# The second layer's attention: weights times values for four token tiles in one product, gate weights loaded block by block

## The chip, the cores and the metric

One Trainium2 chip, one of its cores. The kernel is one launch; its time is the device time of that launch in microseconds. TensorE (PE in the profile) multiplies, VectorE (DVE), ScalarE (ACT) and GpSimd (POOL) do the elementwise work, and SyncE (SP) issues most of the DMAs. Each engine takes its instructions in the order in which the program lists them.

## The reference, cut to what matters

Two layers work on 512 latent and 256 context tokens of width 1024. The change lies in the second layer, which is grouped-query attention with 8 query heads of width 128 and 2 key/value heads:

```
h = rms_norm(x) * (1 + scale) + shift
q, k, v, z = split(h @ w_in)
q, k = rope(rms_norm(q)), rope(rms_norm(k))
p = softmax(q @ k.T * scale)        # per head: 512 queries, 768 keys
o = p @ v                           # per head: 512 x 128
x = x + gate * rms_norm((o * silu(z)) @ w_out)
gate = silu(c) @ ada_w[..., 2D:3D] + b
```

All inputs are float32. The kernel keeps nearly that precision by splitting each factor into a high and a low part and summing three products (high by high, high by low, low by high).

## The kernel before, in words

**Stages of the second layer.** After keys and values are ready, the kernel runs one long stretch in which eight heads of attention, four query projections (`q_proj`, two heads each) and eight gate projections (`z1_proj`, one head each) are interleaved. The projections are the filler: generators in a queue, from which the planner `flow` draws a few products whenever no attention step is due.

**One head.** A *unit* of scores (`s1_units`) takes one tile of 128 tokens. PE makes six products of 384 columns into one of two PSUM buffers, `sc0` and `sc1`. DVE takes the row maximum (L1537) and multiplies it by the query's norm (L1540); ACT exponentiates and sums (L1543); DVE takes the reciprocal of the sum (L1544); POOL scales the tile (L233). The result is a tile of weights `p`, 128 tokens by 768 keys, of which there are 5 buffers.

**Weights times values.** `pv1_steps` works on *two* token tiles at a time (a half, `ch` 0 or 1), so each head goes through it twice. A `tstep` transposes four 128x128 blocks (two token tiles, two key blocks) into one PSUM bank `bk` (L1558); ACT casts them to the high part `ah` (L1561) and DVE forms the low part `al` (L1562). An `mstep` then does the products of this step (`pv_mm`, L167): three terms by two key blocks, six products of 256 columns. Three steps make a half, so a head has 36 such products. At the end of each half ACT copies 128x256 out of the bank (L1575). There are three buffers each of `ah` and `al` (`AB`).

**Banks.** Four banks `bk0` to `bk3` serve projections, transposes and value products in turn; a bank is free again when its reader on ACT or DVE is done.

**Gate.** `gate` of the second layer is formed on DVE: 16 blocks (8 blocks of the inner dimension by two halves of 512 columns) are multiplied by a column of silu(c) and accumulated (L1602, L1604). `gate1_load` fetches two blocks per DMA, 512 KB, into one of two buffers `gw` (L1589); it is issued on SP, where the projections' weights (L223) are issued too. `gate1_finish` sums over the partitions on PE (L406, L407).

**Who sets the order.** Steps have lags and due times (`SLAG1`, `QLAG`, `QTR`, `LA`, `LT`, `LM`, `AT1`, `TS`), a model clock, and priorities (`HOT1`, one per stream). `flow` writes steps in order of their due times; the scheduler below it then orders each engine's queue by priority and readiness.

Of the kernel before, what the change touches and what calls it, by code (L numbers as in the profile page):

```python
# [33 lines left out]
ACD = 0.54  # L34
FILL1 = (('q', 1), ('z', 0), ('z', 2), ('q', 2), ('z', 1), ('q', 3), ('z', 4), ('z', 5), ('z', 3), ('z', 6), ('z', 7))
HOT0 = (4682, 2421, 950, 3759)
HOT1 = (1476, 3151, 2600, 3663, 2938, 0)
WARM = 1817
AGB = 10
PRE = 16.26  # L40
# [13 lines left out]
LT = (1.27, 1.44)  # L54
AHEAD = 2
SLAG = (4.74, 1.08)
SLAG1 = 4.72
AT1 = 12.82
EGL = 'v'
EXS = 'pvvvvv'  # L60
EHF = ('vvvvvvpv', 'pvvvvvvv')
# [6 lines left out]
PRI = (1500, 218, 582, 400)  # L68
GFIN = (10, 13)
QLAG = 2.87  # L70
QTR = 5.35
EG0 = 'v'
EP0 = 'p'
EN1 = 'p'
# [13 lines left out]
def tile_backbone(  # L88
# [1289 lines left out]
    with tc.tile_pool(name="t1", bufs=1, side="right") as t1p:  # L1378
# [126 lines left out]
                pieces(nc.gpsimd, gT1[h], gT1[h], szt1[h], ALU.mult)  # L1505

        def z1_proj(h):
            while not ws.has(12 + h):
                yield None
            wh, wl = ws.get(12 + h)  # L1510
            o = pj(512)
            for kt in range(KT):
                mm3(o, gcols(wh, kt), gcols(wl, kt), h1hi[:, kt, :512], h1lo[:, kt, :512], kt == 0, kt == KT - 1)
                yield 3 * 512 / 2400.0
            ws.release(12 + h)
            sz = t1q.tile([P, 512], F32, tag="sz", name=nm("sz"), bufs=2)
            nc.scalar.copy(sz, o)
            close(o)
            za = t1q.tile([P, 512], F32, tag="za", name=nm("za"), bufs=1)
            silu_parts(sz, za, sz, nc.gpsimd)  # L1520
            szt1[h] = sz
            gate_mul1(h)

        def s1_units(h, ms):
            res = []

            def unit(m):
                g = h // 4
# [8 lines left out]
                nc.vector.tensor_reduce(mx, scv, AX.XY, ALU.max, negate=True)  # L1537
                sr = qrs[h // 2, m][:, h % 2:h % 2 + 1]
                nmx = small()
                nc.vector.tensor_tensor(nmx, mx, sr, ALU.mult)  # L1540
                pt = t1q.tile([P, T], F32, tag="p", name=nm("p"), bufs=5)
                l = small()
                nc.scalar.activation(pt.rearrange("p (j n) -> p j n", j=2), scv, AF.Exp, scale=sr, bias=nmx, accum_out=l)  # L1543
                nc.vector.reciprocal(l, l)  # L1544
                scaled(EN1, pt, pt, l)
                res.append(pt)
# [3 lines left out]
        def pv1_steps(h, at, ch, after, ts, ms):  # L1550
# [31 lines left out]

            chunk(1, tstep, mstep, (0, 2, 4), [after], ts, ms)

        gws = {}

        def gate1_load(half, k2):
            gw = gws[half, k2] = t1q.tile([P, 1024], F32, tag="gw", name=nm("gw"), bufs=2)
            nc.sync.dma_start(  # L1589
                gw.rearrange("p (k n) -> p k n", k=2),  # L1590
                ada_w[1, k2 * 256:(k2 + 1) * 256, 2 * D + half * 512:2 * D + half * 512 + 512].rearrange("(k p) n -> p k n", p=P),
            )

        def gate1_part(half, k2):
            acc = gate1[:, half * 512:half * 512 + 512]
            gw = gws.pop((half, k2))
            with tc.issue_after(last_of(nc.vector)):
                for k in range(2):
                    kt = k2 * 2 + k
                    gs = gw[:, k * 512:(k + 1) * 512]  # L1600
                    if kt == 0:
                        nc.vector.tensor_scalar(acc, gs, scol[:, 0, kt:kt + 1], None, ALU.mult)  # L1602
                    else:
                        nc.vector.scalar_tensor_tensor(acc, gs, scol[:, 0, kt:kt + 1], acc, ALU.mult, ALU.add)  # L1604

        def gate1_finish(half):
            acc = gate1[:, half * 512:half * 512 + 512]
# [38 lines left out]
            add(out_head(o_pre, ghi, glo, w_o[0], OUTC1[0][1]))  # L1646

        at_ = clock[0] + AT1
        qtr = {}
        for h in range(KT):  # L1650
            p, j = h // 2, h % 2
            lag = [(S_[4 * (h - 1) - 1], QLAG)] if h >= 2 else []
            qtr[h] = Step(lambda p=p, j=j: q_tr(p, j), 0.44, lag, ready=lambda p=p: q_t[p] + QTR if p in q_t else None)
            X_.append(qtr[h])
            for ch in range(2):
                at, u = s1_units(h, (2 * ch, 2 * ch + 1))
# [13 lines left out]
        for i in range(8):  # L1670
            if i >= 0:
                Z_.append(Step(lambda i=i: gate1_load(i // 4, i % 4), 0.0, [(S_[1 + i], 0.0)], hot=False))
            if i:
                Z_.append(Step(lambda i=i: gate1_part((i - 1) // 4, (i - 1) % 4), 0.0, [(S_[1 + i + 1], 0.0)], hot=False))
        Z_.append(Step(lambda: gate1_part(1, 3), 0.0, [(S_[1 + 9], 0.0)], hot=False))
# [140 lines left out]
```

## Time and profile before

| | |
|---|---|
| time, median of 3 runs | 792.78 us (792.57 to 792.84) |
| the profiled execution's own time | 792.77 us |
| its span, first to last instruction | 790.8 us |
| lies outside the span | 2.0 us |
| granted TensorE clock | 0.999 |
| PE, DVE, ACT, POOL busy | 98%, 66%, 58%, 41% |
| the second layer's attention, from the first score to the last value product | about 577.4 to 753.2 us |

How to read it: the page is one execution. Busy PE time is the union of overlapping products, so a product's own duration (0.28 us for 256 columns) is longer than the time from its start to that of the next. What a product costs a dense stream is that distance, and the chain of waits gives it: it lists stretches of back-to-back work with their count. A wait of PE appears as "idle before" in the timeline and in the table of waits.

### The profile page before, as it was taken

The page shows a single profiled execution, that of the slowest core. Times are in us where ns is not written, and L with a number is a line of the kernel's source. Part 1 is how long each engine was busy: PE and PEld are TensorE (multiplying, and loading weights), DVE is VectorE, ACT ScalarE, POOL GpSimd, SP SyncE. Part 2 cuts the span into 40 slices and gives each one's busy share as a digit, 9 for nine tenths or more (in the row PEclk, how much of TensorE's full clock was granted, in tenths as well). Part 3 has the DMA queues.
Part 4 walks back from the last instruction along what each step waited for, and adds up shares of the span by engine and source line. Part 5 has one row for each costly group of instructions (what it writes and reads, how often), then busy time and mean ns, then how long its engine had stood idle before and what let it go on. Part 6 is the DMA issues. An engine that isn't in the chain of part 4 may idle for free.

```text
span 790.8 us, 14236 instructions
## 1 busy us (share of the span) xinstructions
PE 776.8 (98%) x5446; PEld 699.2 (88%) x5446; DVE 522.4 (66%) x940; ACT 455.4 (58%) x994; POOL 324.9 (41%) x434
## 2 busy tenths in 40 slices
PE   8999999999999999999999999999999999999996
PEld 6688888988887898888979998899999999989986
DVE  4666677786769637866578753567558977565634
ACT  5546546675575644775468843565456676676632
POOL 1121375663338542353425411585446654234101
PEclk9999999999999999999999999999999999999999
DMA  9934211131422322323330151041423512010102
GB/s 339 384 97 148 80 54 59 50 104 67 138 80 83 118 81 68 120 80 107 117 97 31 51 213 54 1 140 53 159 82 101 153 43 81 27 54 28 54 27 107
DMA packets 35092, 77.77 MB, mean 98 GB/s; under 512 B 3408, under 2 KB 10064, under 8 KB 35024
## 3 DMA queue, kind: packets, MB, share of 16 engines
q1 hardware_dynamic: 31168, 71.05, 26.9%
q10 hardware_dynamic: 3856, 5.81, 2.1%
q8 instruction: 43, 0.70, 0.3%
q14 instruction: 25, 0.20, 0.1%
HBM read 70.56 MB, written 2.10 MB: 92 GB/s over the span
## 4 chain that ended last, share of the span: by engine, by line
PE 89%; DVE 3%; ACT 3%; DMA 2%; POOL 1%; issue 1%; SPq 0%; DVEq 0%; ACTq 0%; POOLq 0%
PE bk L155 56%; PE sc L155 10%; PE bk L167 9%; PE sc L994 5%; PE bk L1059 3%; PE bk L1558 3%; PE bk L835 1%; DMA xnt<-in_xlT 1%; PE sc L1023 1%; POOL wlo L219 1%; DMA raw<-in_b_w 1%; DVE al L1063 1%; PE bk L406 1%; PE bk L407 1%; ACT p L1033 0%
## 5 line engine op out<-in xcount | busy, mean ns | idle before, releaser
L155 PE MATMUL bk<-whi,h 128*128 128x256 f32 (+1 forms) x1184 | 243.7, 299 | 0.0
L155 PE MATMUL bk<-h,whi 128*128 128x512 f32 (+2 forms) x864 | 227.9, 347 | 0.0
L155 PEld LDWEIGHTS bk<-whi,h 128*128 128x128 f32 x1184 | 191.8, 191 | 10.5 <-issue 4.0
L155 PE MATMUL bk<-wlo,h 128*128 128x256 f32 (+1 forms) x592 | 175.7, 299 | 0.0
L155 PEld LDWEIGHTS bk<-h,whi 128*128 128x128 f32 x864 | 149.9, 189 | 17.1 <-issue 2.9
L155 PE MATMUL bk<-h,wlo 128*128 128x512 f32 (+2 forms) x432 | 149.6, 346 | 0.0
L233 POOL TENSOR_SCALAR p<-p,sm 128x768 f32<-128x768 f32 (+1 forms) x80 | 71.7, 899 | 163.1 <-DVE sm L1005 63.9
L155 PEld LDWEIGHTS bk<-wlo,h 128*128 128x128 f32 x592 | 112.6, 191 | 3.8 <-issue 0.7
L219 DVE TENSOR_TENSOR wlo<-raw,whi 128x1024 fp32r<-128x1024 f32 (+1 forms) x66 | 80.7, 1226 | 34.4 <-ACT whi L225 34.3
L155 PEld LDWEIGHTS bk<-h,wlo 128*128 128x128 f32 x432 | 81.5, 189 | 7.1 <-issue 0.2
L225 ACT CAST whi<-raw 128x1024 fp32r<-128x1024 f32 x64 | 67.2, 1050 | 32.9 <-PE bk L155 27.8
L1002 ACT ACTIVATE p<-sc,sm 128x768 f32<-128x768 f32 (+1 forms) x68 | 59.5, 878 | 30.6 <-DVE sm L999 30.1
L999 DVE TENSOR_REDUCE sm<-sc 128x1 f32<-128x768 f32 (+1 forms) x68 | 60.3, 917 | 19.2 <-PE sc L994 19.2
L219 POOL TENSOR_TENSOR sz<-sz,za 128x192 f32<-128x192 f32 (+1 forms) x48 | 35.1, 752 | 65.8 <-ACT za L199 65.7
L1010 DVE SCALAR_TENSOR_TENSOR p<-p,sm,p 128x768 f32<-128x768 f32 (+1 forms) x34 | 40.3, 1186 | 7.4 <-POOL p L233 5.1
L994 PE MATMUL sc<-qk,qk 64*128 64x384 f32 (+1 forms) x396 | 43.8, 351 | 0.7 <-ACT p L1002 0.7
L1562 DVE TENSOR_TENSOR al<-bk,ah 128x512 fp32r<-128x512 f32 x48 | 32.1, 686 | 18.4 <-ACT ah L1561 18.2
L1062 ACT CAST ah<-bk 128x512 fp32r<-128x512 f32 x56 | 31.6, 589 | 19.0 <-PE bk L1059 16.6
L1063 DVE TENSOR_TENSOR al<-bk,ah 128x512 fp32r<-128x512 f32 x56 | 37.4, 683 | 6.7 <-ACT ah L1062 6.5
L1543 ACT ACTIVATE p<-sc,sm,qrs 128x768 f32<-128x768 f32 x32 | 31.9, 996 | 15.1 <-DVE sm L1540 8.9
L994 PEld LDWEIGHTS sc<-qk,qk 64*128 64x128 f32 x396 | 32.8, 184 | 7.7 <-issue 3.4
L1561 ACT CAST ah<-bk 128x512 fp32r<-128x512 f32 x48 | 26.9, 588 | 17.9 <-PE bk L1558 14.6
(240 smaller groups left out, 1492.6 us busy)
## 6 DMA issues: line engine op xcount, KB each, us to landing
raw<-in_a_w SPq DMA_DIRECT2D x28, 512.0 KB, 3.5
araw<-in_ada_w SPq DMA_DIRECT2D x12, 1024.0 KB, 5.2
raw<-in_b_w SPq DMA_DIRECT2D x20, 512.0 KB, 3.5
ag<-in_ada SPq DMA_DIRECT2D x16, 512.0 KB, 7.9
raw<-in_w_out SPq DMA_DIRECT2D x16, 512.0 KB, 3.5
sw<-qr ACTq DMA_DIRECT2D x32, 128.0 KB, 2.1
gw<-in_ada_w SPq DMA_DIRECT2D x8, 512.0 KB, 4.1
xnt<-in_xlT SPq DMA_DIRECT2D x4, 512.0 KB, 5.6
```

What stands on the lines that cost most here:

```text
L155: i = nc.tensor.matmul(o, a, b, start=start, stop=stop)
L167: nc.tensor.matmul(o, v[:, kt + e, c], a[:, e * 256:e * 256 + 256], start=first and i == 0, stop=last and i == 5)
L219: eng.tensor_tensor(dst[:, i:i + n], a[:, i:i + n], b[:, i:i + n], op)
L225: nc.scalar.copy(hi, r)
L233: (nc.vector if eng == "v" else nc.gpsimd).tensor_scalar(dst, src, s_, 1.0, ALU.mult, ALU.mult)
L994: prev = nc.tensor.matmul(sc[m][:, j if nk == T else m, :w], a[r, tok], b[r, c], start=i == 0, stop=i == 2)
L999: nc.vector.tensor_reduce(mx, scv, AX.XY if nk == T else AX.X, ALU.max, negate=True)
L1002: nc.scalar.activation(pv_, scv, AF.Exp, bias=mx, accum_out=l[:, m:m + 1])
L1010: nc.vector.scalar_tensor_tensor(ps_[0], pt, r, ps_[0], ALU.mult, ALU.add)
L1063: nc.vector.tensor_tensor(al, tr, f32(ah), ALU.subtract)
L1543: nc.scalar.activation(pt.rearrange("p (j n) -> p j n", j=2), scv, AF.Exp, scale=sr, bias=nmx, accum_out=l)
L1562: nc.vector.tensor_tensor(al, tr, f32(ah), ALU.subtract)
```

## The change

**Value products.** For heads 0 to 6 a new function, `pv1_wide`, replaces `pv1_steps`. It waits for all four units of the head. A `tstep` transposes one key block of all four token tiles (four blocks of 128x128, as before, L1592) and splits it into `ah` and `al` (L1595, L1596), a step of 128x512 as before; there are six such steps, one per key block. An `mstep` does three products of 512 columns (L1606). A head thus has 18 products of 512 columns in place of 36 of 256, one copy of 128x512 out of the bank (L1609) in place of two of 128x256, and the same 24 transposes, 6 casts and 6 subtractions. Head 7 keeps the two halves.

**Buffers and order.** `p` has 7 buffers instead of 5, since four tiles of a head are held until all are there. A unit now waits in the planner for the last transposes of the head whose `p` buffer it takes over. `z1_proj` does not start while two gated heads are waiting for their attention. The planner's constants move: `HOT1[4]`, `SLAG1`, `AT1`, `QTR`, `LM[1]`.

**Gate loads.** A load is one block, 256 KB, into one of two buffers of half the size. The first two loads are issued ahead of the attention; each further one follows the accumulation of the block whose buffer it takes. The 16 accumulations are the same.

```diff
-HOT1 = (1476, 3151, 2600, 3663, 2938, 0)
+HOT1 = (1476, 3151, 2600, 3663, 3405, 0)
...
-QTR = 5.35
+QTR = 6.73
...
         def z1_proj(h):
-            while not ws.has(12 + h):
+            while not ws.has(12 + h) or sum(g not in done1 for g in szt1) >= 2:
                 yield None
...
-                pt = t1q.tile([P, T], F32, tag="p", name=nm("p"), bufs=5)
+                pt = t1q.tile([P, T], F32, tag="p", name=nm("p"), bufs=7)
...
+        def pv1_wide(h, at, after, ts, ms):
+            g = h // 4
+            st = {}
+
+            def tstep(kt):
+                tr = trp()
+                for i, a in enumerate(at):
+                    nc.tensor.transpose(tr[:, i * P:(i + 1) * P], a[:, kt * P:(kt + 1) * P], ident)
+                ah = t1q.tile([P, 512], F32R, tag="ah", name=nm("ah"), bufs=AB)
+                al = t1q.tile([P, 512], F32R, tag="al", name=nm("al"), bufs=AB)
+                nc.scalar.copy(ah, tr)
+                nc.vector.tensor_tensor(al, tr, f32(ah), ALU.subtract)
+                st[kt] = ah, al
+
+            def mstep(kt):
+                if kt == 0:
+                    st["o"] = pj(512)
+                o = st["o"]
+                ah, al = st[kt]
+                c = slice(g * P, (g + 1) * P)
+                for i, (v, a) in enumerate(((vh, ah), (vl, ah), (vh, al))):
+                    nc.tensor.matmul(o, v[:, kt, c], a, start=kt == 0 and i == 0, stop=kt == NT - 1 and i == 2)
...
+            chunk(1, tstep, mstep, range(NT), [after], ts, ms)
...
-            gw = gws[half, k2] = t1q.tile([P, 1024], F32, tag="gw", name=nm("gw"), bufs=2)
...
+            gw = gws[half, kt] = t1q.tile([P, 512], F32, tag="gw", name=nm("gw"), bufs=2)
+            nc.sync.dma_start(gw, ada_w[1, kt * P:(kt + 1) * P, 2 * D + half * 512:2 * D + half * 512 + 512])
...
-                    if len(T_) >= 6:
-                        st_.lag.append((T_[-4], 0.0))
+                    used = (len(S_) - 7) // 4
+                    if used >= 0:
+                        st_.lag.append((tl[used], 0.0))
...
+        for i in range(2):
+            gate1_load(0, i)
+        for i in range(16):
+            Z_.append(Step(lambda i=i: gate1_part(i // 8, i % 8), 0.0, [(S_[1 + i // 2], 1.5 * (i % 2))], hot=False))
+            if i < 14:
+                Z_.append(Step(lambda i=i: gate1_load((i + 2) // 8, (i + 2) % 8), 0.0, [(Z_[-1], 0.0)], hot=False))
```

Nothing ahead of the second layer's attention moves. Three places within it show how the queues change.

**PE, between heads 4 and 5.** In these rows `p` is a tile of weights, `q` a tile of queries, `sc` a buffer of scores, `h1` with `whi` and `wlo` a product of a gate projection. Before, around the transposes of head 4's second half and the queries' transposes:

```order
L155 MATMUL bk2_70<-h1_687_5281,wlo_1050_7414 128x512
L1558 MATMUL bk0_68<-ident_74,p_1122_7793 128x128
L1494 MATMUL bk1_69<-ident_74,q_1073_7542 128x128
...
L1558 MATMUL bk0_68<-ident_74,p_1128_7843 128x128
L1558 MATMUL bk0_68<-ident_74,p_1122_7793 128x128
L1558 MATMUL bk0_68<-ident_74,p_1128_7843 128x128
L155 MATMUL bk2_70<-h1_687_5281,whi_1049_7413 128x512
L155 MATMUL bk2_70<-h1_688_5282,whi_1049_7413 128x512
L155 MATMUL bk2_70<-h1_687_5281,wlo_1050_7414 128x512
```

The same place in the changed program, where head 3's last steps meet head 4's first (`p_1171` is head 4's fourth tile):

```order
L1606 MATMUL bk2_70<-ah_1167_7938,vl_5916 128x512
L1592 MATMUL bk1_69<-ident_74,p_1171_7952 128x128
L1592 MATMUL bk0_68<-ident_74,p_1139_7789 128x128
L1592 MATMUL bk0_68<-ident_74,p_1145_7818 128x128
L1592 MATMUL bk0_68<-ident_74,p_1150_7840 128x128
L1592 MATMUL bk0_68<-ident_74,p_1171_7952 128x128
L1606 MATMUL bk2_70<-al_1168_7939,vh_5915 128x512
L155 MATMUL sc1_73<-kh_5913,qh_1141_7801 128x384
L155 MATMUL sc1_73<-kl_5914,qh_1141_7801 128x384
```

Gate projections stood between the attention steps before. Now PE's rows 4202 to 4314 hold no projection at all: 30 products of scores (five units), 39 transposes of weights, 8 of queries and 36 value products.

**ACT, at head 2's fourth tile.** `ah` is the cast after a transpose, `za` and `sz` belong to the silu of a gate projection. Before, the exponential of that tile (`p_1057`):

```order
L195 ACTIVATE za_1052_7419<-sz_1051_7417 128x512
L196 ACTIVATE za_1052_7419<-za_1052_7419 128x512
L1543 ACTIVATE p_1057_7457,sm_1058_7458<-sc0_72,sm_1056_7455,qrs_909_6730 128x768
L197 ACTIVATE za_1052_7419<-za_1052_7419 128x512
L1575 COPY g1_1036_7348<-bk1_69 128x256
L1561 CAST ah_1053_7443<-bk0_68 128x512
```

and now (`p_1083`):

```order
L197 ACTIVATE za_1071_7484<-za_1071_7484 128x512
L1595 CAST ah_1063_7455<-bk3_71 128x512
L199 ACTIVATE za_1071_7484<-za_1071_7484 128x512
L1543 ACTIVATE p_1083_7537,sm_1084_7538<-sc0_72,sm_1082_7535,qrs_911_6734 128x768
L1595 CAST ah_1065_7472<-bk3_71 128x512
```

The exponential now stands behind a cast (`ah_1063`) that itself waits for head 1's transposes on PE.

**DVE, at the last gate blocks.** `gw` is a block's buffer, `al` the low part of a step. Before, two accumulations read one buffer:

```order
L1562 TENSOR_TENSOR al_1038_7355<-bk0_68,ah_1037_7354 128x512
L1604 SCALAR_TENSOR_TENSOR gate1_5280<-gw_1005_7214,scol_109,gate1_5280 128x512
L1537 TENSOR_REDUCE sm_1055_7453<-sc0_72 128x1
L1544 RECIPROCAL sm_1044_7388<-sm_1044_7388 128x1
L1604 SCALAR_TENSOR_TENSOR gate1_5280<-gw_1005_7214,scol_109,gate1_5280 128x512
L1562 TENSOR_TENSOR al_1040_7374<-bk3_71,ah_1039_7373 128x512
```

and now each reads its own, with the loads of `gw_1030` and `gw_1042` issued after the 13th and the 14th block (`gw_1011` and `gw_1014`):

```order
L1629 SCALAR_TENSOR_TENSOR gate1_5280<-gw_1014_7207,scol_109,gate1_5280 128x512
L1540 TENSOR_TENSOR sm_1046_7366<-sm_1045_7364,qrs_893_6640 128x1
L1629 SCALAR_TENSOR_TENSOR gate1_5280<-gw_1030_7280,scol_109,gate1_5280 128x512
L1544 RECIPROCAL sm_1048_7369<-sm_1048_7369 128x1
L1498 TENSOR_TENSOR ql_1044_7336<-bk2_70,qh_1043_7335 128x512
L1629 SCALAR_TENSOR_TENSOR gate1_5280<-gw_1042_7328,scol_109,gate1_5280 128x512
L1537 TENSOR_REDUCE sm_1054_7414<-sc1_73 128x1
L1596 TENSOR_TENSOR al_1051_7385<-bk0_68,ah_1050_7384 128x512
```

Behind the last block stand the maximum of head 2's third unit and head 1's first `al`. On SP, weights of later projections are queued behind these loads.

More of the change, by code (lines that the diff above doesn't have):

```diff
@@ L56 @@
 SLAG = (4.74, 1.08)
-SLAG1 = 4.72
-AT1 = 12.82
+SLAG1 = 5.06
+AT1 = 13.45
 EGL = 'v'
@@ L78 @@
 RL = 3.57
-LM = (4.64, 5.5)
+LM = (4.64, 6.57)
 AB = 3
@@ L1583, in pv1_steps @@
             chunk(1, tstep, mstep, (0, 2, 4), [after], ts, ms)
-        gws = {}
-        def gate1_load(half, k2):
-            gw = gws[half, k2] = t1q.tile([P, 1024], F32, tag="gw", name=nm("gw"), bufs=2)
[L1589 to L1594, printed above, removed]
+        def pv1_wide(h, at, after, ts, ms):
[18 more added lines that the diff above has]
+                    nc.tensor.matmul(o, v[:, kt, c], a, start=kt == 0 and i == 0, stop=kt == NT - 1 and i == 2)
+                if kt == NT - 1:
+                    gT1[h] = t1p.tile([P, 512], F32, tag="g1", name=nm("g1"), bufs=8)
+                    (nc.scalar.copy if EG1 == "a" else nc.vector.tensor_copy)(gT1[h], o)
+                    close(o)
+                    done1.add(h)
+                    gate_mul1(h)
+            chunk(1, tstep, mstep, range(NT), [after], ts, ms)
@@ L1595, in gate1_part, with gate1_load @@
+        gws = {}
+        def gate1_load(half, kt):
+            gw = gws[half, kt] = t1q.tile([P, 512], F32, tag="gw", name=nm("gw"), bufs=2)
+            nc.sync.dma_start(gw, ada_w[1, kt * P:(kt + 1) * P, 2 * D + half * 512:2 * D + half * 512 + 512])
+        def gate1_part(half, kt):
             acc = gate1[:, half * 512:half * 512 + 512]
-            gw = gws.pop((half, k2))
+            gs = gws.pop((half, kt))
             with tc.issue_after(last_of(nc.vector)):
[L1598 to L1604, printed above, removed]
+                if kt == 0:
+                    nc.vector.tensor_scalar(acc, gs, scol[:, 0, kt:kt + 1], None, ALU.mult)
+                else:
+                    nc.vector.scalar_tensor_tensor(acc, gs, scol[:, 0, kt:kt + 1], acc, ALU.mult, ALU.add)
@@ L1648, in tile_backbone @@
         at_ = clock[0] + AT1
-        qtr = {}
+        qtr, tl = {}, {}
         for h in range(KT):
@@ L1654, in tile_backbone @@
             X_.append(qtr[h])
-            for ch in range(2):
-                at, u = s1_units(h, (2 * ch, 2 * ch + 1))
+            wide = h < KT - 1
+            for ch in range(1 if wide else 2):
+                at, u = s1_units(h, range(NQ) if wide else (2 * ch, 2 * ch + 1))
                 for i, st_ in enumerate(u):
@@ L1661, in tile_backbone @@
                         st_.lag.append((S_[-2], SLAG1))
-                    if len(T_) >= 6:
-                        st_.lag.append((T_[-4], 0.0))
+                    used = (len(S_) - 7) // 4
+                    if used >= 0:
+                        st_.lag.append((tl[used], 0.0))
                     S_.append(st_)
-                if h == KT - 1 and ch == 1:
+                if not wide and ch == 1:
                     T_.append(Step(tail1, 0.0, [(M_[-1], 0.0), (u[-1], 0.0)]))
-                pv1_steps(h, at, ch, u[-1], T_, M_)
+                if wide:
+                    pv1_wide(h, at, u[-1], T_, M_)
+                    tl[h] = T_[-1]
+                else:
+                    pv1_steps(h, at, ch, u[-1], T_, M_)
         Y_ = [Step(lambda i=i: gate1_finish(i), 0.9, [(S_[GFIN[i]], 0.0)], hot=False) for i in range(2)]
         Z_ = []
[L1670 to L1675, printed above, removed]
+        for i in range(2):
[4 more added lines that the diff above has]
+                Z_.append(Step(lambda i=i: gate1_load((i + 2) // 8, (i + 2) % 8), 0.0, [(Z_[-1], 0.0)], hot=False))
         flow(1, [S_, T_, M_, X_, Z_, Y_])
```

## The prediction

> **What bounds the kernel now.** I began with the page: busy shares, then the chain that ended last.
>
> ```profile
> PE 776.8 (98%) x5446; PEld 699.2 (88%) x5446; DVE 522.4 (66%) x940; ACT 455.4 (58%) x994; POOL 324.9 (41%) x434
> PE 89%; DVE 3%; ACT 3%; DMA 2%; POOL 1%; issue 1%; SPq 0%; DVEq 0%; ACTq 0%; POOLq 0%
> ```
>
> PE is busy for 98% of the span and carries 89% of the chain. Two stretches of the second layer's attention, and the table of waits of PE from 573 to 785 us, say how dense it is there. The columns of the stretches are length, then busy time of PE, PEld, DVE, ACT and POOL with their instructions, granted clock, DMA share, GB/s.
>
> ```profile
> 592.30:660.00 67.70, 67.70 (x504) 66.04 (x503) 58.35 (x113) 44.92 (x103) 39.82 (x48) 1.00 0.31 95
> 660.00:760.00 100.00, 99.56 (x659) 92.28 (x658) 59.56 (x108) 62.67 (x123) 31.02 (x39) 1.00 0.13 43
> ...
> PE sc L155 <- ACT p L1543: 0.4, 1, 0.4
> ```
>
> PE waits once in 212 us. DVE has 9 us to spare in the first 68, so its results come just in time there, yet PE doesn't feel it. So time is won here only by less work on PE, and lost only where PE is made to wait. The timeline of PE shows the one wait (start, duration, what):
>
> ```profile
> 704.75 0.27 PE L1558 MATMUL bk<-ident,p 128*128 128x128 f32 x1
> 705.46 0.44 PE L155 MATMUL sc<-kh,qh 128*128 128x384 f32 x1 [0.44 <-ACT p L1543]
> ```
>
> From the transpose's start to the next product's are 0.71 us; a transpose takes a dense stream 0.11 (below), so PE loses 0.60.
>
> **The products.** What a product costs a dense stream I read from the chain in order of time (start, us, what and how many), and the number of value products from their line:
>
> ```profile
> 643.15 1.91 PE bk L167 x16
> 645.07 0.44 PE bk L1558 x4
> 645.50 1.04 PE sc L155 x6
> 646.78 1.92 PE bk L155 x16
> ...
> 668.28 4.59 PE bk L155 x20
> ...
> 709.76 4.61 PE bk L155 x20
> ...
> L167 PE MATMUL bk<-ah,vh x96: 278/283/367, 606.7 to 752.4; 128*128 128x256 f32 x96
> ```
>
> The 16-fold stretches are products of 256 columns, 1.91 / 16 = 0.1194 and 1.92 / 16 = 0.120 us each; the 20-fold ones have 512 columns, 0.2295 and 0.2305. There are 96 for each of three terms, 288 in eight heads, 36 a head. Seven heads give up 252 x 0.1194 = 30.1 us and get 126 x 0.2295 = 28.9: a gain of 1.2. With the other rows it is 252 x 0.1194 - 126 x 0.2305 = 1.05 to 252 x 0.120 - 126 x 0.2295 = 1.3. It lies on PE, so all of it counts unless a wait eats it. Transposes (0.11 each) and score units (1.04) stay as many.
>
> [...]
>
> The copies out of the bank (two of 128x256 become one of 128x512), the seven `p` buffers and the planner's constants cost PE nothing themselves; ACT is not the bound.
>
> **The old wait.** The 0.60 us hung on an exponential late on ACT for a buffer of scores. The changed order has other neighbours there; I count it as gone, and its like under the new waits.
>
> **New waits.** Three places could make PE wait. The durations, from the groups of the lines between 573 and 785 us and of POOL between 590 and 750 (busy us, mean ns, idle before):
>
> ```profile
> L1543 ACT ACTIVATE p<-sc,sm,qrs 128x768 f32<-128x768 f32 x32 | 31.9, 996 | 15.1 <-DVE sm L1540 8.9 <-PE bk L1558 3.4 <-POOL qrs L1411 2.1
> L1561 ACT CAST ah<-bk 128x512 fp32r<-128x512 f32 x48 | 26.9, 588 | 17.9 <-PE bk L1558 14.6 <-PE bk L167 3.0
> L1543 ACT ACTIVATION_READ_ACCUMULATOR p<-sc,sm,qrs 128x1 f32 x32 | 6.4, 199 | 0.0
> L195 ACT ACTIVATE za<-sz 128x512 f32<-128x512 f32 x8 | 5.1, 639 | 0.2
> ...
> L1562 DVE TENSOR_TENSOR al<-bk,ah 128x512 fp32r<-128x512 f32 x48 | 32.1, 686 | 18.4 <-ACT ah L1561 18.2
> L1537 DVE TENSOR_REDUCE sm<-sc 128x1 f32<-128x768 f32 x32 | 30.4, 949 | 2.0 <-PE sc L155 1.7
> L219 DVE TENSOR_TENSOR wlo<-raw,whi 128x1024 fp32r<-128x1024 f32 x18 | 22.9, 1272 | 13.9 <-ACT whi L225 13.9
> L1540 DVE TENSOR_TENSOR sm<-sm,qrs 128x1 f32<-128x1 f32 x32 | 7.4, 232 | 0.3
> ...
> L1544 DVE RECIPROCAL sm<-sm 128x1 f32<-128x1 f32 x30 | 4.7, 158 | 11.0 <-ACT p L1543 10.9
> ...
> L233 POOL TENSOR_SCALAR p<-p,sm 128x768 f32<-128x768 f32 x31 | 31.9, 1028 | 55.0 <-DVE sm L1544 40.8 <-DVE sm L1540 10.4 <-PE bk L406 3.7
> ```
>
> An engine starts the next instruction before the last has ended. Timelines of ACT and of DVE show by how much:
>
> ```profile
> 664.23 0.60 ACT L1561 CAST ah<-bk 128x512 fp32r<-128x512 f32 x1
> 664.71 1.01 ACT L1543 ACTIVATE p<-sc,sm,qrs 128x768 f32<-128x768 f32 x1
> ...
> 643.57 0.95 DVE L1537 TENSOR_REDUCE sm<-sc 128x1 f32<-128x768 f32 x1
> 644.43 0.68 DVE L1562 TENSOR_TENSOR al<-bk,ah 128x512 fp32r<-128x512 f32 x1
> ```
>
> A cast of 0.60 us holds ACT for 0.48, a maximum of 0.95 holds DVE for 0.86: about 0.1 less than the duration. Each place is bounded by full durations and by these steps.
>
> *The stretch without projections*, PE's rows 4202 to 4314. It is PE work of 5 x 1.04 + 47 x 0.11 + 36 x 0.2295 = 18.6 us, with nothing to fill a wait. ACT's rows for it are 6 exponentials with their sums (7.2), 11 casts (6.5), 2 copies of a cast's size (1.2), 4 activations of the silu (2.6) and one cast of 128x1024 for which I take two of 512 (1.2): 18.7 us, or about 16 with the overlap. DVE has 6 maxima (5.7), 10 `al` and one `ql` (7.5), 11 small ones (2.2), one `wlo` (1.3) and one step of the silu (0.8): 17.5, or 15. At full durations both are as long as PE's work and hand results back and forth; walking the rows I find two waits, 0.3 us at head 4's second transposes (bank 0, for `al_1168`) and 0.6 at its fourth (bank 1, for `al_1189`). With the overlap both vanish, a microsecond to spare. So 0 to 0.9; the overlap is measured, the hand-overs between engines are not in it, and I take 0.4.
>
> *Head 2's fourth tile* (`p_1083`). Its exponential stands on ACT behind `ah_1063`, which needs transposes of head 1. From their end to the fourth tile's transpose, PE has 11 transposes, 5 value products and one unit: 1.2 + 1.15 + 1.04 = 3.4 us. The chain is cast, silu step, exponential, sum, reciprocal, scaling: 0.59 + 0.64 + 1.0 + 0.2 + 0.16 + 1.03 = 3.6, and the first cast starts about 0.2 after the transposes; overlapped it is 3.3 to 3.4. So a wait of 0.1 to 0.4, and the `ah_1065` behind it is late by as much: I take 0.4 for both.
>
> *Gate blocks on DVE.* A DVE instruction that waits for a block holds up the maxima and `al` behind it. I take 0.1 here on the likely case, and make the rest a rival. What else is late on SP (later projections' weights behind the loads) has tens of microseconds.
>
> **The sum.** 792.77 (the profiled execution, 790.8 in its span and 2.0 around it; the median is 792.78) - 1.2 - 0.6 + 0.4 + 0.4 + 0.1 = 790.97 + 0.9 = 791.9 us. A difference under 0.2%, 1.6 us, is about what a measurement of this kernel can't tell from no change; so faster means below 791.2 and slower above 794.4.
>
> **Rivals.**
>
> *No new wait at all.* PE stays as dense as before: 790.97, say 791.0, 0.23% faster. For it speaks that before, with DVE idle for 18 us at the casts (`L1562`'s row), PE still waited only once; the order allows it, with at least 7 us of PE's work between a unit's products and the transposes of its tile. Against it: the stretch without filler has no parallel in the trace. It decides if all waits together stay under 0.2 us or so.
>
> *The gate blocks hold up DVE, and PE with it.* The rows of the loads:
>
> ```profile
> L1604 DVE SCALAR_TENSOR_TENSOR gate<-gw,scol,gate x14: 725/742/1291, 597.6 to 638.5; 128x512 f32<-128x512 f32 x14
> L1589 SPq DMA_DIRECT2D gw<-in_ada_w x8: 368/379/464, 555.6 to 628.0; - x8
> DMA to landing us min/median/max: 3.8/4.1/5.0
> ...
> raw<-in_ada_b SPq DMA_DIRECT2D x4, 256.0 KB, 3.8
> ```
>
> 512 KB land 4.1 us after issue, another tile's 256 KB 3.8. A block is loaded only when the one two places ahead has been accumulated: 0.38 to issue and 3.8 to land, 4.2 us. In DVE's order four instructions lie between the 14th block and the 16th, 0.23 + 0.74 + 0.16 + 0.68 = 1.8 us, so DVE may wait 2.4 there; between the 5th and the 7th are six, about 2.5 us, a wait of up to 1.7. If PE pays both in full, the time is 791.0 + 4.1 = 795.1, slower. It decides where the `al` and maxima behind those blocks are needed sooner than these waits; the rows give them some microseconds, since projections still stand between at these places, and before the change DVE waited long without PE noticing. [...]
>
> *The wide product is no cheaper.* If 512 columns cost just twice 256 in this place, the first term is 0, and the time 791.9 + 1.2 = 793.1: no change. The rows at 643 and 668 us speak against it, though they are of different stretches. [...]
>
> **Chances.** Forecast 0.44, no new wait 0.32, wide product no cheaper 0.06, gate blocks or a like hold-up 0.18. So faster 0.32, same 0.50, slower 0.18. The range of the forecast alone is 790.97 - 0.1 (upper gain) + 0 to 2.3 (all three places at their upper ends, with 1 us for the gate blocks), 790.9 to 793.3. To hold 8 in 10 it has to reach into the rival on either side: 790.7 to 794.6.
>
> **What would show it.** The span's PE order should give 18-fold value products at 0.23 us each in the chain; 126 products of L1606 with 128x512; PE's table of waits in the attention near 0.9 us in all, and naming ACT `ah` or POOL `p` at head 2 and a DVE `al` at heads 4 and 5. I am wrong if the end of the last value product moves by other than -0.9 us against 753.2 (the work behind it is the same), if PE's waits name `gate`, or if DVE stands idle for a DMA `gw` by more than 2 us and PE's gaps follow it.

## The result, and the profile after

The changed kernel takes 795.38 us, median of 6 runs (795.14 to 795.85), beside 792.72 (792.39 to 793.29) for the kernel before on the same chip: a ratio of 1.0034, 95% interval 1.0024 to 1.0044. It is slower by 2.7 us. The profiled span is 793.9 us, 3.1 longer than before's.

The shares by engine and the chain, from the page of after:

```profile
PE 777.3 (98%) x5320; PEld 691.0 (87%) x5320; DVE 521.3 (66%) x940; ACT 454.5 (57%) x987; POOL 324.8 (41%) x434
PE 87%; ACT 3%; DVE 3%; DMA 2%; POOL 2%; issue 2%; SPq 0%; DVEq 0%; ACTq 0%; POOLq 0%
```

PE has 126 products fewer, as planned, and is busy just as long; its share of the chain fell by two points, which went to POOL and to "issue". The two stretches of the attention, then PE's table of waits from 573 to 788 us:

```profile
592.30:660.00 67.70, 65.66 (x426) 59.73 (x425) 55.24 (x107) 41.89 (x96) 39.42 (x48) 1.00 0.36 110
660.00:760.00 100.00, 99.78 (x593) 88.42 (x593) 61.27 (x113) 64.86 (x122) 30.75 (x38) 1.00 0.12 38
```

```profile
PE sc L155 <- ACT p L1543: 1.1, 3, 0.6
PE bk L407 <- POOL ac L405: 0.9, 1, 0.9
```

The loss is in the first stretch. PE was busy for all of its 67.70 us before and lacks 2.04 now, at the same granted clock of 1.00; the second stretch is denser than before's 99.56. The table counts only time in which no product was running. What a wait costs shows in the distance from a product's start to the next one's, less that product's own step in a dense stream (0.109 us for a transpose, 0.120, 0.175 and 0.229 for 256, 384 and 512 columns; dense stretches of before's chain have 0.87 us for 8, 1.92 for 16, 1.05 for 6 and 1.60 for 7 of these). I sum this *excess* from 573 to 790 us. The last transpose ahead of another product often shows some 0.08 us less than its 0.109, and that product as much more (in after four transposes take 0.35 us from 666.76 on and the 512 columns behind them 0.32); in the sum the two nearly cancel, and a dense kernel can come out slightly below zero. It is 0.44 us in before and 4.76 in after. Eight gaps of after hold 3.66 of it (the start is that of the product ahead of the gap):

| start, us | excess, us | PE waits for |
|---|---|---|
| 623.1, 623.7 | 0.17 + 0.42 | cast `ah`; exponential `p` |
| 643.7, 644.4, 645.4 | 0.28 + 0.29 + 0.86 | cast `ah`; `al`; exponential `p` |
| 654.4 | 1.10 | POOL's low part `ac` of the gate's column sum |
| 668.1 | 0.37 | exponential `p` |
| 690.1 | 0.17 | `al` |

The second row is head 2. ACT's timeline there (start, duration, operation, idle before), and PE's:

```profile
640.50 0.59 ACT L1497 CAST qh<-bk 128x512 fp32r<-128x512 f32 x1 [0.85 <-PE bk L1494]
640.99 0.59 ACT L1517 COPY sz<-bk 128x512 f32<-128x512 f32 x1
641.61 0.63 ACT L195 ACTIVATE za<-sz 128x512 f32<-128x512 f32 x1
642.28 0.63 ACT L196 ACTIVATE za<-za 128x512 f32<-128x512 f32 x1
642.94 0.64 ACT L197 ACTIVATE za<-za 128x512 f32<-128x512 f32 x1
643.48 0.57 ACT L1595 CAST ah<-bk 128x512 fp32r<-128x512 f32 x1
644.34 0.63 ACT L199 ACTIVATE za<-za 128x512 f32<-128x512 f32 x1 [0.29 <-DVE za L198]
645.33 0.99 ACT L1543 ACTIVATE p<-sc,sm,qrs 128x768 f32<-128x768 f32 x1 [0.36 <-PE bk L1592]
```

```profile
642.63 1.36 PE L1592 MATMUL bk<-ident,p 128*128 128x128 f32 x11
644.10 0.50 PE L1606 MATMUL bk<-ah,vh 128*128 128x512 f32 x1
644.44 0.40 PE L1606 MATMUL bk<-ah,vl 128*128 128x512 f32 x1
644.96 0.65 PE L1592 MATMUL bk<-ident,p 128*128 128x128 f32 x4
645.37 0.47 PE L1606 MATMUL bk<-al,vh 128*128 128x512 f32 x1
646.46 0.45 PE L155 MATMUL sc<-kh,qh 128*128 128x384 f32 x1 [0.61 <-ACT p L1543]
```

ACT works without a pause from 640.5 to 644.0, three silu steps ahead of the cast. PE has made 11 transposes by then, and its next products need that cast: they start as it ends. Then the exponential waits for transposes of PE, and PE's scores wait for the exponential: each engine stands once for the other.

At 654 us it is POOL, then PE:

```profile
652.24 1.92 POOL L219 TENSOR_TENSOR g<-g,sz 128x256 f32<-128x256 f32 x2 [2.09 <-ACT g L1609]
654.23 1.27 POOL L405 TENSOR_TENSOR ac<-gate,ac 128x512 fp32r<-128x512 f32 x1
```

```profile
654.02 0.60 PE L1592 MATMUL bk<-ident,p 128*128 128x128 f32 x4
655.56 0.50 PE L407 MATMUL bk<-ac,ones_r 128*128 128x512 f32 x1 [0.93 <-POOL ac L405]
```

POOL stands 2.09 us for a head's output, multiplies it by the silu for 1.92, and only then forms the low part for the gate's sum, for which PE waits.

At 623 us the exponential stands on ACT behind a cast that has waited 4.19 us for transposes, at 668 us behind a silu step. ACT's timeline at both places:

```profile
622.70 0.59 ACT L1595 CAST ah<-bk 128x512 fp32r<-128x512 f32 x1 [4.19 <-PE bk L1592]
623.18 1.00 ACT L1543 ACTIVATE p<-sc,sm,qrs 128x768 f32<-128x768 f32 x1
...
667.03 0.64 ACT L195 ACTIVATE za<-sz 128x512 f32<-128x512 f32 x1
667.57 0.99 ACT L1543 ACTIVATE p<-sc,sm,qrs 128x768 f32<-128x768 f32 x1
```

Two rows of the chain show the wide product, and one row of DMA issues the gate loads (count, size, median us from issue to landing):

```profile
679.90 1.15 PE bk L1606 x5
...
709.18 1.82 PE bk L1606 x8
```

```profile
gw<-in_ada_w SPq DMA_DIRECT2D x16, 256.0 KB, 2.8
```

These two stretches cost 0.230 and 0.2275 us a product, as forecast; the median over all 126 is 0.234. A block lands after 2.8 us (median), not 3.8. DVE's table of waits has no row for `gw`.

### The profile page after: what moved, and what is told of

It reads as the page before. It is cut to its first block, busy times and chain, and to the rows that moved or that the text cites. A ratio compares the mean times of both kernels' runs of the same rounds, so it can differ in the third digit from the quotient of the medians.

```text
span 793.9 us, 13999 instructions
## 1 busy us (share of the span) xinstructions
PE 777.3 (98%) x5320; PEld 691.0 (87%) x5320; DVE 521.3 (66%) x940; ACT 454.5 (57%) x987; POOL 324.8 (41%) x434
## 4 chain that ended last, share of the span: by engine, by line
PE 87%; ACT 3%; DVE 3%; DMA 2%; POOL 2%; issue 2%; SPq 0%; DVEq 0%; ACTq 0%; POOLq 0%
PE bk L155 56%; PE sc L155 10%; PE bk L167 5%; PE sc L994 5%; PE bk L1606 3%; PE bk L1059 3%; PE bk L1592 2%; PE bk L835 1%; DMA xnt<-in_xlT 1%; PE sc L1023 1%; POOL wlo L219 1%; DMA raw<-in_b_w 1%; PE bk L407 1%; DVE al L1063 1%; PE bk L406 1%
## 5 line engine op out<-in xcount | busy, mean ns | idle before, releaser
L155 PE MATMUL bk<-whi,h 128*128 128x256 f32 (+1 forms) x1184 | 243.2, 299 | 0.0
L155 PE MATMUL bk<-h,whi 128*128 128x512 f32 (+2 forms) x864 | 227.8, 346 | 0.0
L155 PEld LDWEIGHTS bk<-whi,h 128*128 128x128 f32 x1184 | 191.8, 191 | 10.7 <-issue 3.2
L155 PE MATMUL bk<-wlo,h 128*128 128x256 f32 (+1 forms) x592 | 175.4, 299 | 0.0
L155 PEld LDWEIGHTS bk<-h,whi 128*128 128x128 f32 x864 | 150.1, 189 | 17.1 <-issue 2.9
L155 PE MATMUL bk<-h,wlo 128*128 128x512 f32 (+2 forms) x432 | 149.5, 346 | 0.0
L155 PEld LDWEIGHTS bk<-wlo,h 128*128 128x128 f32 x592 | 112.6, 191 | 4.0 <-issue 0.7
L155 PEld LDWEIGHTS bk<-h,wlo 128*128 128x128 f32 x432 | 81.5, 189 | 7.1 <-issue 0.2
L1062 ACT CAST ah<-bk 128x512 fp32r<-128x512 f32 x56 | 31.6, 589 | 19.1 <-PE bk L1059 16.6
L1063 DVE TENSOR_TENSOR al<-bk,ah 128x512 fp32r<-128x512 f32 x56 | 37.4, 683 | 6.7 <-ACT ah L1062 6.5
L1596 DVE TENSOR_TENSOR al<-bk,ah 128x512 fp32r<-128x512 f32 x42 | 28.1, 684 | 15.4 <-ACT ah L1595 15.1
L1059 PE MATMUL bk<-ident,p 128*128 128x128 f32 x224 | 35.1, 275 | 2.0 <-DVE gate L1133 1.1
```

What stands on the lines that cost most here:

```text
L155: i = nc.tensor.matmul(o, a, b, start=start, stop=stop)
L1059: nc.tensor.transpose(tr[:, e * 256 + i * P:e * 256 + (i + 1) * P], a[:, j * P:(j + 1) * P], ident)
L1063: nc.vector.tensor_tensor(al, tr, f32(ah), ALU.subtract)
```

## The experiments

Each run was timed beside the kernel before on the same chip. The interval of a ratio is about 0.0012 to either side, 1 us, so smaller differences between runs are not read without a trace. Where a run has other buffers, numbers or loads, the planner and the scheduler also write another order; this limits what such a run can tell, and is itself one of the findings.

### Is the wide product cheaper, and does one removed wait pay?

In `half`, the whole-head form stays and each product of 512 columns is issued as two of 256:

```diff
-nc.tensor.matmul(o, v[:, kt, c], a, ...)
+for e in range(2):
+    ce = slice(e * 256, e * 256 + 256)
+    nc.tensor.matmul(o[:, ce], v[:, kt, c], a[:, ce], ...)
```

> The changed kernel with each of the 126 wide products issued as two products of 256 columns, in the same steps. If the wide product saves what the price says (9.3 ns each, 1.2 us in all), this is about 1.2 us slower than the changed kernel: 796.6 us. If the wide product is no cheaper in this place (its median distance in the changed kernel's trace is 0.234 us, two of 256 columns are 0.239), it is at most 0.6 us slower: 795.4 to 796.0.

It took 796.77 us, ratio 1.0053 (1.0040 to 1.0067), against after's 1.0034: 1.5 us more. In the traces PE's last product starts 0.88 us later (788.50 against 787.62), and the attention begins 0.59 earlier (576.85 against 577.44), which makes 1.47 from the first score on. Not all of it is the product: the gaps over 0.15 us hold 4.15 in `half` and 3.66 in after, 0.5 more. By the medians, 0.120 and 0.234, the products themselves give 252 x 0.120 - 126 x 0.234 = 0.8. So the wide product saves 0.8 to 1.5 us; this part of the change works.

In `acv`, DVE and not POOL forms the low part of the gate's sum:

```diff
-nc.gpsimd.tensor_tensor(lo, src, f32(hi), ALU.subtract)
+nc.vector.tensor_tensor(lo, acc, f32(hi), ALU.subtract)
```

> The changed kernel with the low part of the gate's column sum (ac) made on DVE instead of POOL. PE waits 0.9 to 1.1 us for that low part at 654 us of the changed kernel's trace. If that wait is real loss, the time falls by about 1.1 us, to 794.3. If what comes behind was late anyway, or DVE's extra 1.4 us of work pushes the maxima, it stays at 795.4 or rises.

795.30 us, ratio 1.0034 (1.0022 to 1.0047), the same as after. The wait of 1.10 us is gone, and at the same place stand 0.49 for DVE's `ac`, 0.23 for a cast and 0.42 for an exponential; the excess is 4.65. Here the removed wait was passed on to the next engines that were late. ACT's timeline of `acv` at head 2's fourth tile:

```profile
643.22 0.63 ACT L199 ACTIVATE za<-za 128x512 f32<-128x512 f32 x1 [0.43 <-DVE za L198]
644.72 0.99 ACT L1543 ACTIVATE p<-sc,sm,qrs 128x768 f32<-128x768 f32 x1 [0.86 <-PE bk L1592]
```

ACT stands idle for 0.86 us ahead of the exponential, so that no silu step holds it up, and yet PE's gap behind it is 0.86 us, as in after. The same 0.86 stands in `early`, `room7`, `room8`, `room8k` and `oldc`. This gap comes from the exponential's wait for transposes: from those to the next scores PE has one value product, and the exponential takes 0.99.

### Are the score buffers short?

`room8` has eight buffers of scores, and the planner's rule counts eight; to make room, the query tiles have eight buffers in place of nine and an output that nobody reads is bf16. `room7` has that room and seven buffers. `room8k` has eight, and the rule that counts seven.

```diff
-pt = t1q.tile([P, T], F32, tag="p", name=nm("p"), bufs=7)
+pt = t1q.tile([P, T], F32, tag="p", name=nm("p"), bufs=8)
...
-used = (len(S_) - 7) // 4
+used = (len(S_) - 8) // 4
```

> The changed kernel with 8 buffers of p instead of 7 (room made by 8 instead of 9 buffers of q tiles and a bf16 scratch tile for the squares). Theory: three waits of PE for an exponential (1.9 us in all with what follows each) come from a p buffer that is taken again while the head before is still being transposed; with 8 they go and the time is about 793.5. Rival: the exponentials are late because ACT's queue has a cast ahead of them that waits for PE; then 8 buffers change nothing, 795.4.

> Control for the run with 8 buffers of p: 7 buffers as in the changed kernel, but with the same room made (8 buffers of q tiles, bf16 scratch for the squares). Both theories: no change, 795.4, within 0.4.

> Eight score buffers, with the room made as in the run room7, and the planner's rule left as with seven, so that the eighth buffer is only slack at run time. Theory that the exponential of a head's fourth tile waits for a buffer: PE's three waits on ACT p L1543 (0.42, 0.86 and 0.37 us over a product's own step in room7) go, 795.9 - 1.65 = 794.3 us. Rival (ACT's order of casts, silu steps and exponentials makes them, the buffer only gives the last name): the waits come back under the name of a cast or stay, 795.3 us or more.

They took 799.24 us (1.0083, 1.0069 to 1.0097), 795.93 (1.0043, 1.0030 to 1.0056) and 795.80 (1.0040, 1.0027 to 1.0053); `room7`, the control, is 0.5 above after, a little outside the 0.4 that was expected but inside the intervals. The theory of the eighth buffer falls: it gains nothing, and with the rule changed it costs 3.3 us against `room7`, at new places. ACT's timeline of `room8k` has the same wait, on another exponential:

```profile
645.68 0.99 ACT L1543 ACTIVATE p<-sc,sm,qrs 128x768 f32<-128x768 f32 x1 [0.45 <-PE bk L1592]
```

The scheduler used the slack to put an exponential of the next head there, which again needs the buffer that these transposes free. PE's loss behind it is 0.86 us as before.

In the other direction, `p6` has six buffers (and a rule that counts six), and `pairs6` six buffers and before's loads of two blocks; `w6old` is before with nothing but the whole-head form, its z condition and six buffers, so it keeps before's loads and planner numbers. From after to `p6`:

```diff
-pt = t1q.tile([P, T], F32, tag="p", name=nm("p"), bufs=7)
+pt = t1q.tile([P, T], F32, tag="p", name=nm("p"), bufs=6)
...
-used = (len(S_) - 7) // 4
+used = (len(S_) - 6) // 4
```

> After with six score buffers in place of seven. If waiting for a score buffer is what costs, waits grow: 796.5 to 799 us. If the order as a whole costs, anything between 794 and 799, at other places than after's. It is the partner of the run pairs6.

> The run p6 with before's loads of two gate blocks and their turn. Theory (the single blocks cost within the wide form what they cost alone in half chunks, 2.3 us): 2 us or more below p6. Rival (the form costs, whatever the loads): within 1 us of p6.

> Before with the wide form of seven heads, its z condition and six score buffers, and neither the new gate loads nor the new planner numbers. Theory (the form itself is cheap, loads and numbers bring the waits): excess under 1 us and 126 cheaper products, 791 to 792.3 us. Rival (the form brings them, or any order that the numbers were not fitted to): 794.5 to 800.

801.32 us (1.0111, 1.0097 to 1.0125), 801.17 (1.0107, 1.0091 to 1.0122) and 800.81 (1.0107, 1.0093 to 1.0120). `p6` and `w6old` lie above every range that was given. Six buffers cost 6 us more than after's seven (`p6`); `p6`, `pairs6` and `w6old` agree, so with six buffers neither the loads' size nor the numbers make a difference that these runs can tell. The largest gap, 2.48 us, is the same in all three. ACT's timeline of `p6` and then PE's:

```profile
729.57 3.22 ACT L1652 CAST h<-g 128x512 fp32r<-128x512 f32 x6 [0.60 <-PE bk L155]
732.70 1.04 ACT L225 CAST whi<-raw 128x1024 fp32r<-128x1024 f32 x1
733.65 0.58 ACT L1517 COPY sz<-bk 128x512 f32<-128x512 f32 x1
```

```profile
731.57 0.47 PE L1606 MATMUL bk<-al,vh 128*128 128x512 f32 x1
734.28 0.66 PE L1592 MATMUL bk<-ident,p 128*128 128x128 f32 x4 [2.24 <-ACT sz L1517]
```

Seven casts stand on ACT ahead of the copy that empties the bank which the next transposes need. It is again ACT's order.

### Where does the form cost, and which other part costs?

`late` has the whole-head form in heads 4 to 6 alone, `early` in heads 0 to 3 alone; everything else is after's (a unit waits for the last transposes of the tile whose buffer it takes). The edit of `late` is below; `early` has `h < 4`.

```diff
-wide = h < KT - 1
+wide = 4 <= h < KT - 1
```

> The wide form only for heads 4 to 6; heads 0 to 3 and 7 in half chunks, everything else (7 score buffers, single gate blocks, the planner's numbers) as after. Theory (the waits come with the wide form where projections and their silu share ACT and DVE with it, heads 0 to 3): the waits at 622 to 668 us go, the old wait at 704 stays away, 54 products of 512 columns save 0.5 us; 792.5 - 0.5 - 0.6 + about 0.4 = 791.8 us, between 791.0 and 793.0. Rival one (the planner's numbers or the gate blocks, not the form): the waits before 670 us stay and the time is 794.5 or more. Rival two (the form costs at every head alike): about 3/7 of 4.3 us of waits, 794.

> The wide form only for heads 0 to 3; heads 4 to 7 in half chunks, everything else as after. Theory (the waits belong to the wide form of heads 0 to 3): 72 products of 512 columns save 0.7 us, the waits at 622 to 668 us stay at about 4 us, with a wait of up to 0.6 us back at 704; 792.5 - 0.7 + 4.0 = 795.8 us, between 794.8 and 796.8. Rival (the stretch without projections is what costs): under 793.

`early` took 795.59 us (1.0036, 1.0023 to 1.0048), with the gaps of after up to 668 us to within 0.02 us and an excess of 4.20: heads 4 to 6 add 0.56 of excess in after, about what their 54 cheaper products save, and so nothing to the loss, in line with the second stretch of the profile. `late` missed by far: 799.77 us (1.0093, 1.0077 to 1.0108), an excess of 8.5 with gaps of 1.82, 0.64, 0.75 and 0.52 us between 631 and 644, where it has half chunks. So the form is not the only thing that makes PE wait there. The next runs take the other parts one by one, in the kernel before: `single` has only the single gate blocks, `bz` only the condition of `z1_proj`, `bnum` only the planner's numbers (five, though the expectations say six); `b7` is `single` with seven score buffers. `oldc` is after with before's numbers. The edit of `bz`:

```diff
-while not ws.has(12 + h):
+while not ws.has(12 + h) or sum(g not in done1 for g in szt1) >= 2:
```

> After with the six numbers of the planner that the diff changes (HOT1, SLAG1, AT1, QTR, LM's second) put back to their values of before. Theory (the form brings the waits): waits of PE of at least 3 us remain in the attention, if at other places, and the time is 794.5 to 798. Rival (the new numbers bring them): under 1 us of waits, 791.5 to 792.5.

> Before with nothing changed but the gate loads and sums, in single blocks with after's rule for their turn. PE's order changes in the second layer, since the blocks are steps of the planner. Theory one (the wide form itself brings the waits): PE's excess over the products' own steps stays at 0.4 to 1 us, 792.5 to 793.3. Theory two (any change of the planned order brings waits, because the numbers fit one order only): excess of 1.5 to 8 us, 794 to 800.

> Before with nothing changed but the waiting condition of z1_proj (no third projection of z until a head is done). Theory one (the wide form): 792.5 to 793.3, excess under 1 us. Theory two (any change of the order): 794 to 800; it is the smallest change of order of the four (828 lines of difference on PE), so the smallest excess of them, 1 to 4 us.

> Before with the six numbers of the planner of after, nothing else. Theory one (the wide form): 792.5 to 793.3. Theory two (the order): excess of 2 to 8 us, 794.5 to 800, with waits at 620 to 670 us like those of the run late, which has the same numbers and half chunks for heads 0 to 3.

> The run single with seven score buffers in place of five, and the release rule of the run late. Theory one (the wide form) and a cover of buffers: 792.3 to 793, no wait at 704 us. Theory two (the order): 794 to 800. If single is slow and this is not, buffers were what single lacked.

| run | us | ratio (95%) | excess, us |
|---|---|---|---|
| oldc | 796.42 | 1.0048 (1.0035 to 1.0060) | 5.8 |
| single | 794.96 | 1.0029 (1.0017 to 1.0040) | 2.9 |
| bz | 792.06 | 0.9992 (0.9984 to 1.0001) | -0.3 |
| bnum | 801.96 | 1.0117 (1.0103 to 1.0131) | 10.1 |
| b7 | 795.68 | 1.0041 (1.0027 to 1.0055) | 3.5 |

`oldc`, `single` and `b7` came out where the ranges for waits brought by the form or by the order had them, `bnum` above its range and `bz` below both of its own. The new numbers are worth about 1 us in after (`oldc` against after, at the edge of the intervals) and cost 9 in the kernel before: here they fit one order only. `late`, which has them with half chunks in heads 0 to 3, is in line with that; no run has them with half chunks everywhere and after's other parts. `bz` refutes that *any* change of the order costs: it has no gap over 0.15 us at all. And `single` alone loses 2.3 us. There the forecast's second rival, the gate blocks, does come true. DVE's timeline, then SP's, ACT's and PE's:

```profile
624.17 0.75 DVE L1598 SCALAR_TENSOR_TENSOR gate<-gw,scol,gate 128x512 f32<-128x512 f32 x1 [1.68 <-DMA gw<-in_ada_w]
624.84 0.15 DVE L1540 TENSOR_TENSOR sm<-sm,qrs 128x1 f32<-128x1 f32 x1
624.91 1.22 DVE L219 TENSOR_TENSOR wlo<-raw,whi 128x1024 fp32r<-128x1024 f32 x1
```

```profile
626.16 0.33 SPq L223 DMA_DIRECT2D raw<-in_b_w  x1
```

```profile
630.49 1.05 ACT L225 CAST whi<-raw 128x1024 fp32r<-128x1024 f32 x1 [3.15 <-DMA raw<-in_b_w]
631.45 0.99 ACT L1543 ACTIVATE p<-sc,sm,qrs 128x768 f32<-128x768 f32 x1
```

```profile
632.58 0.44 PE L155 MATMUL sc<-kh,qh 128*128 128x384 f32 x1 [1.07 <-ACT p L1543]
```

A block comes late, and behind it on DVE `wlo`, whose end frees the buffer for the next projection's weights. These are issued at 626.16 (623.73 in before); ACT's cast stands 3.15 us for them, behind the cast an exponential, and behind that PE's scores. Four engines pass one late block on, each by its order. `single3` gives the blocks a third buffer:

```diff
-gw = gws[half, kt] = t1q.tile([P, 512], F32, tag="gw", name=nm("gw"), bufs=2)
+gw = gws[half, kt] = t1q.tile([P, 512], F32, tag="gw", name=nm("gw"), bufs=3)
```

> The run single with three buffers for the gate blocks. In single, ACT waited 3.2 us at 627 to 630 us for projection weights that stood on SP behind gate loads, and DVE 1.3 us at 630 to 632 for a block; PE waited 1.2 and 0.7 us behind them. Theory (the loads' queue on SP and the blocks on DVE are the cost): these waits go, 792.5 to 793.5 us. Rival (the order of PE and ACT): the waits take other names, 794.3 or more.

793.73 us, ratio 1.0015 (1.0006 to 1.0024), between the two ranges: about half of the loss is back. The weights are issued at 624.56, ACT waits 1.8 us for them in place of 3.2, and PE's gaps there are 0.40 and 0.69 in place of 1.24 and 0.66.

### The price of the form alone

`bz7` is `oldc` with half chunks in all heads, and the same buffers, loads, numbers and z condition. `mid` is `bz` with the whole-head form in heads 4 and 5 and six buffers; PE's order is that of `bz` up to head 3. From `oldc` to `bz7`:

```diff
-wide = h < KT - 1
+wide = False
```

> The run oldc (796.4) with half chunks in all heads in place of the wide form: seven buffers, single blocks, the new z condition, before's numbers. Theory one (the form brings the waits): 2 us or more below oldc, at most 794.4. Theory two (what costs is an order that the numbers don't fit, whatever the form): within 1.2 us of oldc, 795.2 to 797.6, like b7 (795.7), which lacks only the z condition.

> The run bz (792.1) with the wide form in heads 4 and 5 alone and six score buffers; PE's order is that of bz up to the end of head 3. If the wide form is cheap where the order before it stays tight: 36 products save 0.34 us, new waits at most 0.5, 791.6 to 792.3 us, the fastest of all. If any change of the order costs: waits of 1 us or more behind 680 us, 793 to 796.

`bz7` took 794.36 us (1.0022, 1.0012 to 1.0031), so the form costs 2.1 us net, just what the first theory asked and outside the second's range. PE's waits of `bz7`, then of `oldc`:

```profile
PE sc L155 <- ACT p L1543: 0.8, 2, 0.6
PE bk L1558 <- DVE al L1562: 0.6, 1, 0.6
```

```profile
PE sc L155 <- ACT p L1543: 1.0, 3, 0.6
PE bk L1606 <- DVE al L1596: 0.9, 1, 0.9
PE bk L1606 <- ACT ah L1595: 0.2, 1, 0.2
```

The excess is 1.9 us in the one and 5.8 in the other: the form adds 4.0 of excess, of which 2.1 remain in the time. The products take back 1.4, by the steps that the excess is counted from (252 x 0.120 - 126 x 0.229); the other 0.5 is that the attention begins so much earlier in the trace of `oldc` (577.03 against 577.52).

`mid` missed the hoped-for best version: 795.80 us (1.0035, 1.0022 to 1.0048). Up to 690 us it is dense; then PE waits 0.51 us for the copy of a gate projection and 1.50 for an exponential, in heads whose form added nothing to the loss in after, where no gate projection lay between them. Three of its five executions also have a lower granted clock (last section); the other two took 794.2. No version beat both kernels beyond doubt: `bz` is 0.6 us below before, and its interval just reaches it.

## Why the prediction was wrong, point by point

- *The products, -1.2.* Right in kind and near in size: 0.8 to 1.5 in `half`. The rows behind the 1.2 were of projections (L155); in its own place the wide product takes 0.234 us, not 0.2295. The third rival is refuted all the same: the saving is not zero. By the prediction's rows one product of 512 columns costs 9.3 ns less than two of 256 (2 x 119.4 - 229.5), by the medians in its own place about 6 (2 x 120 - 234).
- *The old wait, -0.6.* Right: after has no gap at 704. But the form did not remove it: `early` has half chunks in those heads, `bz` everywhere, and neither has the gap. `bz` changes the condition of `z1_proj` alone.
- *The stretch without projections, +0.4.* The one gap there holds 0.17, at 690.1; the excess of the whole stretch, 679.7 to 698.8 us, is 0.46. So the size was right, and most of it lies in small pieces, not in the two waits that I had walked.
- *Head 2's fourth tile, +0.4.* The right place, but another wait and a mis-sized term: 1.43 us with the two gaps ahead of it. I counted a chain from the cast to the scaling by POOL, for the fourth tile's transposes; PE waits for a cast, an `al` and the exponential instead. Three silu steps hold ACT for 1.9 us ahead of the cast, which bears on the first two gaps (0.57). The third, 0.86, is as long in `acv`, where ACT was idle: the exponential waits for the transposes, which I had left out.
- *The gate blocks, +0.1.* No wait for a block in after, so the price was right; the row that I used, 3.8 us to land, was not, since it was 2.8. The rival itself was real: it cost 2.3 us in `single`, by way of the weights' loads, which I had set aside with "tens of microseconds". It does not act in after's order.
- *"Three places could make PE wait."* This is the step that failed. There are five, and those I had not walked (623, 654 and 668 us) hold 2.06 us, a term that the sum had at nothing; with head 2's they make the change of sign. The sentence that the seven buffers and the planner's constants cost PE nothing themselves failed with it: they change the order, and alone they moved the time by 6 us (`p6`) and 9 (`bnum`). All but the one at 654 us have a trait in common in the traces: the six steps of a head follow one upon another, and each hands over to ACT and DVE and back, so that a cast or an exponential that stands behind a silu step, a weight cast or a wait for transposes has no other value products to cover it. The rows show such queues at 623, 644 and 668 us; that the form makes PE wait more at equal other parts is measured by `bz7` against `oldc`; that the crowding of a head's steps is the reason is read from the rows and was not tested by itself.
- *The rest.* Gaps over 0.15 us explain 3.06 of the 4.32 us of added excess; 1.26 lie in smaller ones, which I had priced at nothing. About half of that is L1606 itself, by its 0.234 us: 126 x 0.0045 = 0.6 against the 0.2295 that I used. I had said that the last value product would end 0.9 us earlier with the same work behind it. It ends 1.9 later and the span is 3.1 longer, so the work behind it is not the same: 197 products stand there, 190 before.

One chain of single steps from before to after, by the runs: single blocks +2.3, seven buffers +0.7, z condition -1.3, the form +2.1, the numbers -1.0, in all +2.7 (rounded). Other chains give other prices: by way of six buffers (`w6old`, `pairs6`, `p6`, after) they are +8.2, +0.4, +0.2 and -5.9. Each price is a difference of two medians and known to 1 us or a little more, so those under 1.5 us are not shown one by one. But the large ones suffice: the loss is no one part's. What the form costs holds for one set of the other parts, and whether numbers fitted once more would win its 1.2 us stays open.

## What to carry to other kernels

Where an engine is busy for 98% and never waits, a part that makes fewer, larger products saves its own small gain and risks the cover (here 1.4 us of products by their steps, against 4.0 of excess, `bz7` to `oldc`): before trusting a gain of 1 us, walk *every* place where the busy engine takes back a result, and count what stands ahead of that result in the other engine's queue, and what that result waits for in turn, not its own chain alone. Do not price the parts of such a change one by one: buffers, loads and planner numbers fit one order, and the same numbers were worth about 1 us in after and cost 9 in the kernel before. When an experiment takes one wait away, look at what stands at the same place afterwards, before counting it as won.

## What the runs showed of the hardware that was not expected

In some executions a wait of PE is followed by a drop of the granted clock. Stretches of `p6`, `w6old` and `late` (length, busy time of PE, PEld, DVE, ACT and POOL, granted clock, DMA share, GB/s):

```profile
731.00:735.00 4.00, 1.76 (x12) 1.30 (x11) 4.00 (x8) 4.00 (x8) 0.00 (x0) 1.00 0.00 0
735.00:739.00 4.00, 3.75 (x14) 3.17 (x14) 3.61 (x8) 3.27 (x8) 0.92 (x1) 0.57 0.34 100
739.00:743.00 4.00, 4.00 (x25) 3.50 (x24) 3.05 (x9) 2.60 (x6) 1.31 (x2) 1.00 0.09 33
```

```profile
731.00:735.00 4.00, 1.76 (x12) 1.26 (x11) 4.00 (x8) 4.00 (x8) 0.00 (x0) 1.00 0.01 2
735.00:739.00 4.00, 3.75 (x19) 2.84 (x20) 3.81 (x9) 3.97 (x9) 1.68 (x2) 1.00 0.33 117
```

```profile
631.00:634.00 3.00, 1.34 (x7) 1.10 (x8) 3.00 (x5) 1.57 (x3) 0.00 (x0) 0.90 0.32 94
634.00:638.00 4.00, 4.00 (x23) 3.98 (x22) 2.50 (x6) 1.57 (x3) 1.27 (x1) 0.65 0.57 193
```

After a wait of 2.5 us in `p6` the granted clock is 0.57 from 735 to 739 us, and 0.50 from 736 to 738. After one of 1.8 in `late` it is 0.90 and 0.65 in the two stretches above. `mid` shows the same from 694 to 698 us, at 0.61, and at 0.50 from 696 to 698, after waits of 0.5 and 1.5 us. Some 1.7 us of full clock are missing each time (0.43 x 4 in `p6`, 0.10 x 3 + 0.35 x 4 in `late`, 0.39 x 4 + 0.03 x 4 in `mid`, which has 0.97 from 698 to 702). By my estimate the drop makes the work of a busy PE longer by these 1.7 us: two value products (`vl` by `ah`) at 696.2 and 697.5 us of `mid` last 0.63 us each, against a median of 0.395 in after. In `w6old` the same wait, at the same time, leaves the clock at 1.00. Nor does it come in every execution of one kernel: the two executions of `mid` with a mean clock of 0.999 took 794.2 us, the three with 0.997 took 795.8 to 796.3; those of `p6` and `pairs6` took 800.5 to 801.0 us at 0.998 or 0.999 and 801.6 to 802.0 at 0.996, and one execution of `w6old` at 0.996 took 801.9, the others 800.5 to 800.9. By these times I estimate that the drop costs these kernels about 1 to 2 us, which is part of what they lost; where it lies only the profiled executions show. In `late`, 799.8 us at 0.997 stands beside 799.6 to 800.7 at 0.999: no cost is seen there. Ahead of these drops PE was idle for no more than 2.5 us at a time; what decides whether the clock drops after a wait, these runs do not show.
